# Hybrid decoder layer on one core: four z tiles of the first branch move between the memory's key products, and the token combinations and the first pair's weights are made beside them

## The chip, the cores and the metric

The kernel runs on one core of a Trainium2 chip. The metric is the device time of one execution in microseconds; of several runs the median counts. The core has an engine for matrix products (PE, with its weight loads as PEld), a vector engine (DVE), a scalar engine (ACT), a general engine (POOL), and SP, which here issues all DMA transfers, in order.

## The reference, cut to what matters

The layer normalises 1024 tokens of width 1024 to `h` and multiplies `h` by one wide matrix `w_in`. Its columns feed three branches: a gated delta rule over chunks (8 heads), a causal attention with two maps per head (8 heads), and an attention into a fixed memory of 256 rows (4 heads). The parts that the change touches:

```python
(gdn_qkv, gdn_a, gdn_b, gdn_z, dq, dk, dv, dz, mq, mz, gate_logits) = [h @ w_in[:, lo:hi] for lo, hi in bounds]
...
oa = gated_delta_rule_chunked(qa, ka, va, g, beta)
oa = rms_norm(oa, gdn_norm_w) * jax.nn.silu(gdn_z.reshape(b, s, GDN_HEADS, GDN_DV))
...
m = rms_norm(mem, mem_norm_w)
mk, mv = jnp.split(m @ w_mem_kv, 2, axis=-1)
```

After the branches, gates merge them, an output product and a last normalisation follow, and `x` is added.

## The kernel before, in words

All products are made in float32 precision out of halves: every operand is split into a rounded part (hi) and the rest (lo), and each product is three passes: hi by hi, hi by lo, lo by hi.

**Weights.** `wsplit` (L159) takes a raw tile of 128x512 (tag `wr`, three buffers), lets SP load it (L163, 256 KB), casts it on ACT (L165, tag `wh`, two buffers) and subtracts on DVE (L167, tag `wl`, two buffers). Every weight outside the paired products goes through these buffers, one after the other: this text calls the three of `wr` the ring.

**Stage 1, up to L709.** The delta rule. Inside `with gx:` two pools, `yp` and `gp`, hold its tiles. `gemm` (L207) makes a tile of 128 columns by 1024 tokens in 48 matmuls out of two raw tiles. Beside the gemms run Python generators: `spawn` adds one, `tick` advances each by a step, and `count` ticks after every six matmuls. `scan` (L632) is the recurrence, three steps per chunk, eight chunks, two heads at a time; after it POOL normalises (L689, L690) and `channels` (L244) transposes the result to a tile `os[n]`. `zmul(n)` (L263) makes z tile n with a gemm, takes silu on ACT (L267), multiplies `os[n]` by it (L270) and stores it. Tiles 0 to 5 stand here, with their silu in a `yt` tile of pool `yp`; then `flush` ends all generators, and `gx` closes.

**Stage 2, L711 to L1024.** A new pool `xp` takes the place of the closed ones: its tiles exist only when those of `yp` and `gp` are given up. `mem_norm` (L735) loads the memory, normalises and transposes it into hi and lo tiles. Beside it `zmul(6)` and `zmul(7)` run. `combine_tokens` (L802) makes, in four rounds, the sums and differences of token blocks that Strassen's scheme needs (L808 to L817) and splits them (L732, L733), in tiles of tags `hi`, `lo`, `o` and `q`; the tiles `os[n]` are of tag `q` too, eight buffers. Then come 8 key tiles (`mem_keys`, L767: two raw tiles each, 12 matmuls of 256 columns per raw tile), whose results are stored (L1016), and `mem_values` (L778) for f = 0 and f = 1: 8 raw tiles each, 6 matmuls of 512 columns per raw tile, and the results are split from PSUM and stored by eight DMAs after each f (L1023).

**Stage 3, from L1028.** `strassen` (L876) makes the rest of the wide product in pairs of column tiles, seven products per pair instead of eight. `Pair.load` (L834) loads raw weights, `Pair.upper` (L841) makes a weight sum on DVE (L850, in a tile of the ring) and casts it (L852), `Pair.lower` (L854) subtracts (L856), `Pair.multiply` (L858) does the matmuls. Before its loop it loads the first pair and makes three uppers and two lowers: products 1, 5 and 6. The sum for product 6 uses that for 5, and the sum for product 3, made in the loop, reads that for 6. Attention runs as a generator beside it. PSUM accumulators of stage 2 are given up and new banks opened (L1291) before the pairs.

**What sets the order.** The order of the text is a priority. Each engine's queue is put in order when the kernel is built: of what is ready by the builder's own clock, the instruction first in the text goes first, and one further down goes where the others are not ready or their buffers not free. On the chip each queue then runs strictly in that order.

Of the kernel before, what the change touches and what calls it, by code (L numbers as in the profile page):

```python
# [19 lines left out]
KT = D // P  # L20
NT = S // P
H = 8
# [7 lines left out]
C_Z = 3088  # L30
# [20 lines left out]
def hybrid_layer_kernel(  # L51
# [124 lines left out]
    def spawn(gen):  # L176
        threads.append(gen)
# [85 lines left out]
    def zmul(n, zcol, tile_):  # L263

        pz = gemm(w_in, zcol + n * P, hh, hl)
        sz = tile_()
        A.activation(sz, pz, AF.Silu)  # L267
        until(lambda: n in os)
        o = os.pop(n)
        V.tensor_tensor(o, o, sz, op=ALU.mult)  # L270
        nc.sync.dma_start(oscr[0][n], o)


    with gx:
# [428 lines left out]
        for step, h in ((key, 0), (key, 1), (key, 2), (key, 3), (qry, 0), (val, 0), (qry, 1), (val, 1),  # L703
                        (val, 2), (key, 4), (val, 3), (key, 5), (qry, 2), (key, 6), (qry, 3), (key, 7),
                        (val, 4), (val, 5), (qry, 4), (qry, 5), (val, 6), (val, 7), (qry, 6), (qry, 7)):
            step(h)
        for n in range(6):
            zmul(n, C_Z, yt)
        flush()  # L709

# [24 lines left out]
    def mem_norm():  # L735

        mts = []
        for t in range(2):
            mt = rtile((P, D))
            nc.sync.dma_start(mt, mem[t * P:(t + 1) * P, :])  # L740
            mts.append(mt)
        for _ in range(2):
            mh.append(xtile((P, 4, MEM), F32R))
            ml.append(xtile((P, 4, MEM), F32R))
        sq = rtile()
        for mt in mts:
            ss = small([P, 1], "ss", 4)
            A.activation(sq, mt, AF.Square, accum_out=ss)
            rs = small([P, 1], "rs", 4)
            rpow(rs, ss, 1.0 / D, EPS, mhalf)  # L750
            V.tensor_scalar(mt, mt, rs, None, op0=MUL)
            yield
        for k2 in range(4):
            pt = sd()
            for kk in range(2):
                for t in range(2):
                    T.transpose(pt[:, 2 * kk + t], mts[t][:, (2 * k2 + kk) * P:(2 * k2 + kk + 1) * P], ident)
            for kk in range(2):
                k = 2 * k2 + kk
                src = pt[:, 2 * kk:2 * kk + 2].rearrange("p a b -> p (a b)")  # L760
                A.activation(mh[k // 4][:, k % 4], src, AF.Copy, scale=memw[:, k:k + 1])
                V.scalar_tensor_tensor(ml[k // 4][:, k % 4], src, memw[:, k:k + 1],
                                       mh[k // 4][:, k % 4].bitcast(F32), op0=MUL, op1=SUB)
            yield
        ready.add("mem")

    def mem_keys(n, mk):  # L767
        pm = acc()
        for j in range(2):
            hi, lo = wsplit(wcols(w_kv, j, n * P))  # L770
            for kk in range(4):
                T.matmul(pm[:, :MEM], lhsT=hi[:, kk], rhs=mh[j][:, kk], start=(j + kk == 0), stop=False)
                T.matmul(pm[:, :MEM], lhsT=hi[:, kk], rhs=ml[j][:, kk], start=False, stop=False)
                T.matmul(pm[:, :MEM], lhsT=lo[:, kk], rhs=mh[j][:, kk], start=False, stop=(j == 1 and kk == 3))
                count(2)
        split(mk[0][:, n % 4], mk[1][:, n % 4], pm[:, :MEM])
# [25 lines left out]
    def combine_tokens():  # L802

        for j in range(4):
            (b1, (u0, u1)), (b2h, b2l) = lower[j], upper[j]
            b11, b12, b21, b22 = (hit((P, 512), F32) for _ in range(4))
            f32 = lambda t: t.bitcast(F32)
            V.tensor_tensor(b11, f32(b1[:, 0]), f32(b1[:, 1]), op=ADD)  # L808
            V.tensor_tensor(b12, f32(u0[:, :]), f32(u1[:, :]), op=ADD)
            for b, sl in ((b21, slice(0, 512)), (b22, slice(512, 1024))):  # L810
                V.tensor_tensor(b, f32(b2h[:, sl]), f32(b2l[:, sl]), op=ADD)
            yield
            t2 = lot((P, 512), F32)
            V.tensor_tensor(b11, b12, b11, op=SUB)
            V.tensor_tensor(t2, b22, b11, op=SUB)
            V.tensor_tensor(b12, b22, b12, op=SUB)
            V.tensor_tensor(b21, b21, t2, op=SUB)  # L817
            yield
            for p, src, new in ((5, b11, ot), (6, t2, ot), (7, b12, qt), (4, b21, qt)):
                t = new((P, 2, 512), F32R)  # L820
                split(t[:, 0], t[:, 1], src)
                comb[p].append((t[:, 0], t[:, 1]))
                yield

    ORDER = (1, 5, 6, 2, 7, 3, 4)

# [47 lines left out]
                self.put(i, f, ps, self.kept.get(add))  # L874

    def strassen(pairs):  # L876
        seq = [(q, p) for q in pairs for p in ORDER]

        def upper(n):
            if n < len(seq):  # L880
                seq[n][0].upper(seq[n][1])

        def lower(n):
            if n < len(seq):
                seq[n][0].lower(seq[n][1])

        pairs[0].load(True)
        pairs[0].load(False)
        upper(0)
        lower(0)  # L890
        upper(1)
        lower(1)
        upper(2)
        for n, (q, p) in enumerate(seq):
            if p in (1, 6) and n + 7 < len(seq):
                seq[n + 7][0].load(p == 1)
            lower(n + 2)
            upper(n + 3)
            q.multiply(p)
# [78 lines left out]
    def key_query(h):  # L978
        return Pair((C_DK + h * P, C_DQ + h * P),
                    gathered(lambda i, f, t: spawn((queries_apart if i else keys_apart)(h, f, t))))  # L980

    def values_pair(h):
        def done(i, f, t):
            nc.sync.dma_start(vd[h + i][:, half[f]], t)
            mark("v", h + i)
        return Pair((C_DV + h * P, C_DV + (h + 1) * P), gathered(done))
# [11 lines left out]
    def silu_z(bi, col, n):  # L998
        return Pair((col + n * P, col + (n + 1) * P), through(True, szd[bi][n:n + 2], ("sz", bi, n // 2)))

    def gates(bi, n):
        c = C_G + bi * D + n * P
        return Pair((c, c + P), through(False, gts[bi][n:n + 2], ("gate", bi, n // 2)))

    spawn(mem_norm())
    zmul(6, C_Z, xtile)
    zmul(7, C_Z, xtile)
    until(lambda: "mem" in ready)
    spawn(combine_tokens())
    for n in range(2):  # L1010
        mk = [xtile((P, 4, MEM), F32R) for _ in range(2)]
        for i in range(4):
            mem_keys(4 * n + i, mk)
        for h in range(2):
            for u in range(2):
                nc.sync.dma_start(mkd[2 * n + h][:, :, u], mk[u][:, 2 * h:2 * h + 2].bitcast(F32))  # L1016
    mv = [[xtile((P, D), F32R) for _ in range(2)] for _ in range(2)]
    for f in range(2):
        mem_values(f, mv)
        for h in range(2 * f, 2 * f + 2):  # L1020
            for t in range(2):
                for u in range(2):
                    nc.sync.dma_start(mvd[h][:, t, u], mv[t][u][:, h * MEM:(h + 1) * MEM].bitcast(F32))  # L1023
# [253 lines left out]
        ready.add("attention")  # L1277
        yield from make0

    pairs = []  # L1280
    for h in range(H):
        pairs.append(key_query(h))
        pairs.append(silu_z(1, C_DZ, h - 1) if h % 2 else values_pair(h))
    for h in range(4):
        pairs.append(mem_query(h))
        pairs.append(silu_z(2, C_MZ, 2 * h))
    pairs += [gates(b, n) for b in range(3) for n in range(0, KT, 2)]

    spawn(attention())
    pace[0] = 2  # L1290
    new_banks()  # L1291
    strassen(pairs)
    new_banks()
    ready.add("pairs")
    pace[0] = 6
# [68 lines left out]
    pw = xtile()  # L1364
    nc.sync.dma_start(pw, post_w.to_broadcast([P, D]))

    def products(po, t, ks, f):
        ts_ = slice(t * P, (t + 1) * P)
        for k in ks:
            for lt, rt in ((yh, wh), (yh, wl), (yl, wh)):  # L1370
                T.matmul(po[f], lhsT=lt[k][:, ts_], rhs=rt[k][f],  # L1371
                         start=(k == 0 and lt is yh and rt is wh), stop=(k == 7 and lt is yl))
# [4 lines left out]
    pos = {t: columns() for t in range(2)}  # L1377
    for t in range(2):
        for f in range(2):
            products(pos[t], t, range(4), f)  # L1380
    for t in range(NT):

        ts_ = slice(t * P, (t + 1) * P)
        po = pos[t] if t < 2 else columns()
        xr, res = xtile(), xtile()
        nc.sync.dma_start(xr, x[ts_, :])
        ss = small([P, 2], "oss", 4)
        for f, sl in enumerate(half):
            products(po, t, range(4 if t < 2 else 0, KT), f)
            A.activation(res[:, sl], po[f], AF.Square, scale=1.0 / 32, accum_out=ss[:, f:f + 1])  # L1390
        rs = small([P, 1], "rs", 4)
        V.tensor_scalar(rs, ss[:, 0:1], ss[:, 1:2], EPS, op0=ADD, op1=ADD)
        G.tensor_tensor(rs, rs, mhalf[:, 0:1], op=ALU.pow)
        for f, sl in enumerate(half):
            V.scalar_tensor_tensor(res[:, sl], po[f], rs, pw[:, sl], op0=MUL, op1=MUL)
            (V if f else G).tensor_tensor(res[:, sl], res[:, sl], xr[:, sl], op=ADD)
            nc.sync.dma_start(out[ts_, sl], res[:, sl])
# [24 lines left out]
```

## Time and profile before

| what | value |
|---|---|
| median of 3 runs | 1966.76 us (1961.39 to 1967.66) |
| the profiled execution's own time | 1959.28 us |
| its span, first to last instruction | 1957.3 us |
| PE busy | 1889.6 us of the span |
| mean granted clock of TensorE | 0.993 of full |

The profile is of one execution, which took 1959.28 us, 0.4% under the median; 2.0 us of it lie outside the span. All times of the trace below count from the span's start. The stages touched lie between 505 and 627 us.

### The profile page before, as it was taken

The page shows a single profiled execution, that of the slowest core. Times are in us where ns is not written, and L with a number is a line of the kernel's source. Part 1 is how long each engine was busy: PE and PEld are TensorE (multiplying, and loading weights), DVE is VectorE, ACT ScalarE, POOL GpSimd, SP SyncE. Part 2 cuts the span into 40 slices and gives each one's busy share as a digit, 9 for nine tenths or more (in the row PEclk, how much of TensorE's full clock was granted, in tenths as well). Part 3 has the DMA queues.
Part 4 walks back from the last instruction along what each step waited for, and adds up shares of the span by engine and source line. Part 5 has one row for each costly group of instructions (what it writes and reads, how often), then busy time and mean ns, then how long its engine had stood idle before and what let it go on. Part 6 is the DMA issues. An engine that isn't in the chain of part 4 may idle for free.

```text
span 1957.3 us, 28521 instructions
## 1 busy us (share of the span) xinstructions
PE 1889.6 (97%) x10231; PEld 1561.1 (80%) x10231; DVE 1261.3 (64%) x2578; ACT 931.1 (48%) x2057; POOL 140.5 (7%) x115
## 2 busy tenths in 40 slices
PE   7999999999988999999999999999999999999998
PEld 5778888788875787878887878888878777888886
DVE  6787678754395687878877777766666653434532
ACT  5544554554363565656655555655444551212211
POOL 1230131302101000000000000000000000000011
PEclk9999999999999999999999999999999999999999
DMA  4323131321264646555555354443476477665522
GB/s 126 95 85 101 43 91 52 102 64 55 83 197 143 200 150 205 153 180 158 183 157 172 113 158 162 143 151 108 162 235 201 146 240 254 202 206 165 159 86 86
DMA packets 292609, 282.44 MB, mean 144 GB/s; under 512 B 40066, under 2 KB 224756, under 8 KB 292468
## 3 DMA queue, kind: packets, MB, share of 16 engines
q1 hardware_dynamic: 292468, 280.63, 45.9%
q8 instruction: 80, 1.31, 0.3%
q14 instruction: 61, 0.50, 0.1%
HBM read 189.27 MB, written 91.29 MB: 143 GB/s over the span
## 4 chain that ended last, share of the span: by engine, by line
PE 77%; DVE 8%; DMA 5%; issue 5%; ACT 3%; POOL 2%; SPq 1%; DVEq 0%; POOLq 0%; ACTq 0%
PE bank L866 30%; PE acc L217 9%; PE acc L222 9%; PE acc L218 9%; PE sd L1154 3%; PE sd L1108 2%; PE sd L1109 2%; PE sd L1142 2%; PE sd L1213 1%; DMA x<-mqd 1%; PE sd L1371 1%; DMA wr<-in_w_mem_kv_dram 1%; PE sd L472 1%; DVE u L973 1%; DVE wl L167 1%
## 5 line engine op out<-in xcount | busy, mean ns | idle before, releaser
L866 PE MATMUL bank<-h,hi 128*128 128x512 f32 x864 | 284.9, 402 | 2.8 <-DVE x L733 2.8
L217 PE MATMUL acc<-h,wh 128*128 128x512 f32 x548 | 225.2, 412 | 4.4 <-DVE y L435 3.0
L165 ACT CAST wh<-wr 128x512 fp32r<-128x512 f32 x144 | 89.3, 620 | 285.2 <-PE acc L218 247.0
L218 PE MATMUL acc<-h,wh 128*128 128x512 f32 x548 | 215.6, 394 | 0.0
L866 PE MATMUL bank<-o,hi 128*128 128x512 f32 x576 | 190.7, 404 | 1.6 <-ACT u L871 1.5
L866 PE MATMUL bank<-q,hi 128*128 128x512 f32 x576 | 189.9, 403 | 2.3 <-DVE u L921 2.2
L866 PEld LDWEIGHTS bank<-h,hi 128*128 128x128 f32 x864 | 160.6, 189 | 35.9 <-issue 3.2
L222 PE MATMUL acc<-h,wl 128*128 128x512 f32 x548 | 181.8, 394 | 0.6 <-DVE wl L167 0.6
L866 PE MATMUL bank<-h,lo 128*128 128x512 f32 x432 | 173.5, 402 | 0.0
L167 DVE TENSOR_TENSOR wl<-wr,wh 128x512 fp32r<-128x512 f32 x144 | 103.7, 722 | 105.7 <-ACT wh L165 99.7
L852 ACT CAST hi<-wr 128x512 fp32r<-128x512 f32 x144 | 89.3, 620 | 125.5 <-PE bank L866 124.6
L856 DVE TENSOR_TENSOR lo<-wr,hi 128x512 fp32r<-128x512 f32 x144 | 99.8, 693 | 56.5 <-PE bank L866 48.6
L866 PEld LDWEIGHTS bank<-q,hi 128*128 128x128 f32 x576 | 107.0, 189 | 25.2 <-DVE u L921 2.6
L866 PEld LDWEIGHTS bank<-o,hi 128*128 128x128 f32 x576 | 107.4, 190 | 24.0 <-ACT u L871 2.4
L217 PEld LDWEIGHTS acc<-h,wh 128*128 128x128 f32 x548 | 103.4, 189 | 23.2 <-issue 4.4
L222 PEld LDWEIGHTS acc<-h,wl 128*128 128x128 f32 x548 | 102.7, 188 | 22.7 <-DVE wl L167 1.3
L218 PEld LDWEIGHTS acc<-h,wh 128*128 128x128 f32 x548 | 103.6, 189 | 16.9 <-DVE h L733 0.3
L866 PE MATMUL bank<-o,lo 128*128 128x512 f32 x288 | 116.4, 404 | 0.0
L866 PE MATMUL bank<-q,lo 128*128 128x512 f32 x288 | 115.7, 402 | 0.0
L1124 ACT ACTIVATE x<-x,ng 128x256 f32<-128x256 f32 (+7 forms) x128 | 98.7, 774 | 31.8 <-DVE ng L1120 31.4
L852 ACT CAST hi<-raw 128x512 fp32r<-128x512 f32 x108 | 67.0, 620 | 75.0 <-PE bank L866 72.6
L866 PEld LDWEIGHTS bank<-h,lo 128*128 128x128 f32 x432 | 81.7, 189 | 16.3
(361 smaller groups left out, 4048.4 us busy)
## 6 DMA issues: line engine op xcount, KB each, us to landing
raw<-in_w_in_dram SPq DMA_DIRECT2D x144, 256.0 KB, 3.6
wr<-in_w_in_dram SPq DMA_DIRECT2D x64, 256.0 KB, 2.9
qd<-u SPq DMA_DIRECT2D x64, 256.0 KB, 3.1
wl<-qd SPq DMA_DIRECT2D x64, 256.0 KB, 3.7
gts<-u SPq DMA_DIRECT2D x48, 256.0 KB, 3.3
u<-oscr SPq DMA_DIRECT2D x48, 256.0 KB, 4.7
raw<-gts SPq DMA_DIRECT2D x24, 512.0 KB, 4.4
o<-gscr SPq DMA_DIRECT2D x16, 512.0 KB, 4.4
```

The costliest lines, as they stand in the source:

```text
L165: A.copy(hi, raw)
L167: V.tensor_tensor(lo, raw, hi.bitcast(F32), op=ALU.subtract)
L217: T.matmul(ps[:, sl], lhsT=hi[:, kk], rhs=hh(k, f), start=(k == 0), stop=False)
L218: T.matmul(ps[:, sl], lhsT=hi[:, kk], rhs=hl(k, f), start=False, stop=False)
L222: T.matmul(ps[:, sl], lhsT=lo[:, kk], rhs=hh(k, f), start=False, stop=(k == 7))
L852: A.copy(self.hi[p], self.src[p])
L856: V.tensor_tensor(self.lo[p], self.src[p], self.hi[p].bitcast(F32), op=SUB)
L866: T.matmul(ps, lhsT=t[l][:, kk], rhs=comb[p][kk][r], start=(first and kk + n == 0), stop=(kk == 3 and n == 2), skip_group_check=True)
L1108: T.matmul(ps[m], lhsT=q4[:, m], rhs=ks[m][:, u:e], start=True, stop=False)
L1109: T.matmul(ps[m], lhsT=q4[:, 2 + m], rhs=ks[m][:, u:e], start=False, stop=True)
L1124: A.activation(s[i][m][:, :w], s[i][m][:, :w], AF.Exp, bias=ng[:, m:m + 1], scale=scl, accum_out=l)
L1154: T.matmul(po[:, 0], lhsT=pT[:, c], rhs=vt[:, c], start=(c == 0), stop=(c == i))
```

## The change

The z tiles 4 and 5 leave stage 1: they come after `gx` has closed, beside `mem_norm` and the token combinations, with their silu in an `xp` tile. Tile 6 comes after the second of the eight key tiles, tile 7 after the sixth. `combine_tokens` starts with `mem_norm`, but its round j waits until no more than 6 - 2j tiles `os[n]` are left, since it needs their buffers. `strassen` becomes a generator that stops once after its preparation, and is called up to there between the value products of f = 0 and f = 1; the list of pairs moves up for that. The products' own count is the same. A helper `products` near the end is renamed `out_products`.

```diff
@@ stage 1
-        for n in range(6):
+        for n in range(4):
             zmul(n, C_Z, yt)
         flush()
@@ combine_tokens
         for j in range(4):
+            while len(os) > 6 - 2 * j:
+                yield
...
                 comb[p].append((t[:, 0], t[:, 1]))
                 yield
+        ready.add("tokens")
@@ strassen
         upper(1)
         lower(1)
         upper(2)
+        yield
         for n, (q, p) in enumerate(seq):
@@ stage 2
     spawn(mem_norm())
-    zmul(6, C_Z, xtile)
-    zmul(7, C_Z, xtile)
+    spawn(combine_tokens())
+    zmul(4, C_Z, xtile)
+    zmul(5, C_Z, xtile)
     until(lambda: "mem" in ready)
-    spawn(combine_tokens())
     for n in range(2):
         mk = [xtile((P, 4, MEM), F32R) for _ in range(2)]
         for i in range(4):
             mem_keys(4 * n + i, mk)
+            if i == 1:
+                zmul(6 + n, C_Z, xtile)
...
     for f in range(2):
+        if f:
+            until(lambda: "tokens" in ready)
+            products = strassen(pairs)
+            next(products)
         mem_values(f, mv)
@@ stage 3
     spawn(attention())
     pace[0] = 2
     new_banks()
-    strassen(pairs)
+    for _ in products:
+        pass
     new_banks()
```

## Rows read from the trace of the kernel before

**Rows 1.** The page's part 1: busy time, share of the span, instructions.
```profile
PE 1889.6 (97%) x10231; PEld 1561.1 (80%) x10231; DVE 1261.3 (64%) x2578; ACT 931.1 (48%) x2057; POOL 140.5 (7%) x115
```

**Rows 2.** Stretches, 504.7 to 626.6 us: length, then each engine's busy time, clock.
```profile
core 0: us, PE busy (x) PEld busy (x) DVE busy (x) ACT busy (x) POOL busy (x), PEclk, DMA share, GB/s
...
504.70:533.40 28.70, 28.70 (x153) 24.23 (x152) 8.42 (x19) 10.26 (x26) 7.50 (x4) 1.00 0.24 74
533.40:558.00 24.60, 23.56 (x111) 19.15 (x110) 23.10 (x40) 13.92 (x26) 1.87 (x2) 1.00 0.63 193
558.00:586.20 28.20, 24.13 (x184) 22.10 (x182) 26.46 (x46) 15.91 (x31) 0.00 (x0) 1.00 0.67 205
586.20:601.60 15.40, 13.87 (x58) 9.92 (x59) 9.75 (x16) 6.73 (x12) 0.00 (x0) 1.00 0.59 173
601.60:619.90 18.30, 13.12 (x49) 8.40 (x48) 12.03 (x20) 8.43 (x15) 6.40 (x4) 1.00 0.56 178
619.90:626.60 6.70, 3.91 (x9) 3.15 (x10) 1.98 (x3) 1.16 (x2) 0.00 (x0) 0.50 0.46 159
```

**Rows 3.** PE's waits, 533.4 to 623 us: total, times, longest.
```profile
PE acc L785 <- ACT wh L165: 4.6, 4, 2.3
PE bank L866 <- DVE x L733: 2.8, 1, 2.8
PE acc L786 <- DVE nlam L1038: 2.1, 1, 2.1
```

**Rows 4.** Timeline of DVE, chunks of the scan: start, length, line, operation, tiles, count.
```profile
492.31 0.35 DVE L651 SCALAR_TENSOR_TENSOR v<-sd,negeG,v 128x128 f32<-128x128 f32 x1 [2.11 <-PE sd L648]
...
498.91 0.35 DVE L651 SCALAR_TENSOR_TENSOR v<-sd,negeG,v 128x128 f32<-128x128 f32 x1 [1.98 <-PE sd L648]
```

**Rows 5.** Timeline of POOL after the last scan.
```profile
517.04 1.64 POOL L689 TENSOR_TENSOR sso<-sso,mhalf 128x8 f32<-128x8 f32 x1 [45.05 <-DVE sso L688]
...
522.80 1.90 POOL L690 TENSOR_TENSOR v<-v,sso 128x1024 f32<-128x1024 f32 x1
```

**Rows 6.** Timeline of DVE, from z tile 5 to the normalised memory.
```profile
534.30 1.23 DVE L270 TENSOR_TENSOR q<-q,y 128x1024 f32<-128x1024 f32 x1 [0.23 <-ACT y L267]
...
535.63 0.69 DVE L808 TENSOR_TENSOR hi<-h 128x512 f32<-128x512 f32 x1
...
552.19 0.48 DVE L762 SCALAR_TENSOR_TENSOR x<-sd,cols,x 128x256 fp32r<-128x256 f32 x1
```

**Rows 7.** Timeline of PE: two products of a key tile, two of a value tile.
```profile
558.00 0.28 PE L772 MATMUL acc<-x,wh 128*128 128x256 f32 x1
558.12 0.28 PE L773 MATMUL acc<-x,wh 128*128 128x256 f32 x1
...
591.26 0.39 PE L785 MATMUL acc<-wh,x 128*128 128x512 f32 x1
591.49 0.40 PE L786 MATMUL acc<-wl,x 128*128 128x512 f32 x1
```

**Rows 8.** Chain of waits, one turn of the ring: start, length, what.
```profile
590.20 3.98 DMA wr<-in_w_mem_kv_dram
594.28 0.63 ACT wh L165
594.93 0.70 DVE wl L167
595.65 3.22 DMA wr<-in_w_mem_kv_dram
```

**Rows 9.** Timeline of SP's queue, 594 to 612 us.
```profile
595.65 6.06 SPq L163 DMA_DIRECT2D wr<-in_w_mem_kv_dram  x5
...
602.46 3.87 SPq L1023 DMA_DIRECT2D mvd<-x  x8
606.37 1.42 SPq L163 DMA_DIRECT2D wr<-in_w_mem_kv_dram  x3
```

**Rows 10.** Timeline of DVE in the value products of f = 1.
```profile
613.99 1.52 DVE L856 TENSOR_TENSOR lo<-wr,hi 128x512 fp32r<-128x512 f32 x1
```

More of the change, by code (lines that the diff above doesn't have):

```diff
@@ L1003, in gates @@
         return Pair((c, c + P), through(False, gts[bi][n:n + 2], ("gate", bi, n // 2)))
+    pairs = []
+    for h in range(H):
+        pairs.append(key_query(h))
+        pairs.append(silu_z(1, C_DZ, h - 1) if h % 2 else values_pair(h))
+    for h in range(4):
+        pairs.append(mem_query(h))
+        pairs.append(silu_z(2, C_MZ, 2 * h))
+    pairs += [gates(b, n) for b in range(3) for n in range(0, KT, 2)]
     spawn(mem_norm())
-    zmul(6, C_Z, xtile)
-    zmul(7, C_Z, xtile)
+    spawn(combine_tokens())
+    zmul(4, C_Z, xtile)
+    zmul(5, C_Z, xtile)
     until(lambda: "mem" in ready)
-    spawn(combine_tokens())
     for n in range(2):
@@ L1278, in attention @@
         yield from make0
[L1280 to L1287, printed above, removed]
     spawn(attention())
@@ L1365, in hybrid_layer_kernel, with out_products @@
     nc.sync.dma_start(pw, post_w.to_broadcast([P, D]))
-    def products(po, t, ks, f):
+    def out_products(po, t, ks, f):
         ts_ = slice(t * P, (t + 1) * P)
@@ L1379, in hybrid_layer_kernel @@
         for f in range(2):
-            products(pos[t], t, range(4), f)
+            out_products(pos[t], t, range(4), f)
     for t in range(NT):
@@ L1388, in hybrid_layer_kernel @@
         for f, sl in enumerate(half):
-            products(po, t, range(4 if t < 2 else 0, KT), f)
+            out_products(po, t, range(4 if t < 2 else 0, KT), f)
             A.activation(res[:, sl], po[f], AF.Square, scale=1.0 / 32, accum_out=ss[:, f:f + 1])
```

## The prediction

> **What bounds the kernel now.** I read the busy shares first: PE is busy 97% of the span [rows 1], so the change can only win PE's idle time, or time at the half clock. Then I cut the span into stretches around the edited lines [rows 2]. The reader is to see that PE is full from 504.7 to 533.4 (z tiles 4 and 5 beside the end of the last scan), idle 1.0 us in the next 24.6 (z tiles 6 and 7, the memory's normalisation), and then idle 4.1, 1.5 and 5.2 us in the key products, in the value products of f = 0 and in those of f = 1. In the last stretch TensorE's granted clock is 0.50, its 1.2 GHz level, right after such gaps. DVE is nearly full from 533.4 to 586.2. The waits say what PE lacks: the cast of the next weight tile, a lo part behind other DVE work, and, at the change to the pairs, the splitting of the last value tile [rows 3].
>
> Two pitches turn this into losses. A key product follows the last by 0.12 us, a value product by 0.23 [rows 7]; so the 12 products of a raw key tile take 1.44 us and the 6 of a raw value tile 1.40. From 558.0 to 601.6 there are 16 raw key tiles and 8 raw value tiles: 23.0 + 11.2 = 34.2 us of work in 43.6, a loss of 9.4. From 601.6 to 619.9 there are 8 more: 11.2 in 18.3, a loss of 7.1.
>
> One turn of the ring is a load of about 3.4 us (3.98 in the row; the chain's next is 3.2), an issue of 0.33, a cast of 0.63 and a subtraction of 0.70 [rows 8], some 5.05. With three raw tiles that is 1.68 us per tile, already more than PE's 1.4; the measured pitch is 43.6 / 24 = 1.82.
>
> **The change, part by part.** No product is added or removed.
>
> A. Tiles 4 and 5 leave stage 1. The work of 504.7 to 533.4 stays on PE: tile 4's products are free to fill the gaps of the last scan, since only their silu needs the new pool. What moves is the pool's gate. Now it opens when tile 5's product with `os` ends at 535.5, and DVE's first token sum starts 0.1 us later [rows 6]. Then it opens after the last scan: POOL needs 7.66 us from its first power to its last product [rows 5], and the transposes that read the result about 1 us. The scan's two last chunks run at 6.6 us each [rows 4], of which 18 z products at 0.23 are 4.1. Bounds for the tail: as now (POOL starts at 517.0), or 5.4 us earlier if the chunks shrink to their own chain of some 3.9 us (an estimate: six hops, PE and DVE in turn, of two instructions of about 0.3 us each); I take the middle, 514.3, because fillers still stand between the steps. So the gate opens at 523.0 (520.3 to 525.7), 12.5 us earlier than now. But the memory's tiles take 17.1 us from the gate, 535.5 to 552.7 [rows 6], and nothing but tiles 4 and 5 covers them: PE's work up to the end of the first key tile is 533.4 + 1.3 (transposes) + 2.9 = 537.6, and that tile cannot end before 523.0 + 17.1 + 0.4 = 540.5. A new wait of 2.9 us, less the 1.0 that goes: **+1.9 us** (-0.8 to +4.6). Queued behind it on PE are the key products, and nothing else is ready, since tile 6's weights come behind theirs in the ring.
>
> B. Tiles 6 and 7 between the keys. A z tile's two raw tiles keep PE 24 x 0.23 = 5.5 us each, so behind it the ring stands full: one tile split and three raw, four in stock. The runs without z are 4, 8 and 12 tiles long (keys 0-1; 2-5; 6-7 and f = 0); beyond the stock lie 0 + 4 + 8 = 12 tiles, each losing 1.82 - 1.42 = 0.40: a loss of 4.8 against 9.4, **-4.6 us**. Bounds: by the ring's own turn alone (1.68) the loss is 3.1, a gain of 6.3; with a stock of two, 18 tiles lose 7.2, a gain of 2.2. The token sums (32 sums and 16 splits in four rounds) lie beside it: two rounds under tiles 4 and 5, where DVE is busy 8.4 of 28.7 us [rows 2], the third by tile 6, the fourth beside keys 6 and 7. I cost them at nothing; without that cover they would come back as late lo parts. The Trainium skill, page "Perfetto Trace Analysis", section "Optimization Strategy", says that stages with different most-contended engines may gain by being interleaved; taken alone it would give all 9.4 us back and a sum of -3.9. The ring's turn speaks against that beyond the stock.
>
> C. The first pair's preparation, moved in front of f = 1. Its two sums use the ring, and the sum for product 6 is kept until the sum for product 3 is made, inside the pair loop and behind all of f = 1 in the ring. So f = 1 has two raw tiles. Now five loads go out from 595.65 to 601.7, four of them for f = 1, before eight stores hold SP from 602.46 to 606.3 [rows 9]. Then the two slots that come free first go to the sums, and the loads start at about 599.2 and 600.4: the first product is at 603.6 (2.0 late), the next two loads wait for the stores until 606.4 (PE idle 4.0 to 610.4), and after that each pair of tiles needs a turn of 4.7 us: pairs start at 615.1 and 619.8, the end is at 622.6 instead of 619.9, **+2.7 us**. In it the wait of 2.1 us [rows 3], for a lo part behind the pair's own lo part [rows 10], is gone. Bounds: the loads of f = 1 take their slots first and that wait goes with some of the others, -3.2; or every tile costs half a turn, 8 x 2.5 + 3.9 = 23.9, +5.6. What DVE did at 611 to 619 is not missed later: the wait for the banks (2.8) [rows 3] stays, as the last value tile is split as before.
>
> D. Clock. The half clock after 619.9 costs (626.6 - 619.9 - 2.8) / 2 = 2.0 us [rows 2, 3] and stays. New gaps, in A and C, can bring another such stretch; 6.7 us at half clock cost at most 3.3. I take **+0.9**, 0 to 3.3.
>
> Sum: 1.9 - 4.6 + 2.7 + 0.9 = +0.9 us. On the profiled execution, 1959.3 becomes 1960.2; that execution is 7.5 us under the median, and the median's 1966.8 becomes **1967.7**. 0.3% is 5.9 us, about what a measurement of this kernel can tell from no change.
>
> **Rivals.**
>
> 1. *The interleaving works in full.* The ring is full whenever PE needs it, the memory is ready in time, and f = 1 keeps its loads: -0.8 - 6.3 - 3.2 = -10.3, 1956.5. For it: DVE is full exactly where PE waits now [rows 2], and half of DVE's load moves away. Against: the ring's turn and the slots of C. It is what the Trainium skill's rule on interleaving, named in B, would promise.
>
> 2. *The ring with one tile held becomes the bound of f = 1.* Place: the eight loads of f = 1. Price: +5.6 of C's upper end and, as PE idles half the time, a half clock of +3.3; with A and B as taken 1.9 - 4.6 + 5.6 + 3.3 = +6.2, 1973.0. It decides once f = 1 takes more than about 23 us from its first product's due time to its last. For it: the held sum has no other place. Against: if the loads overtake the sums, nothing is held. The Trainium skill, same page and section, says that the same gap repeating can mean that buffers for the next tile are missing. Here the gaps of 2.3 us and less in front of the casts [rows 3] fit that, and the change takes a buffer away.
>
> 3. *It doesn't do what it says.* The queues are put in order by readiness, so tile 6 or 7 may be drawn out from between the keys; then B gives nothing and the sum is +5.5, 1972.3, at the edge of what can be told.
>
> **How the numbers follow.** My forecast's chance is 0.33, rival 1 has 0.31, rival 2 0.28, rival 3 0.08. Rival 1 lies below -5.9 us: faster 0.31. The forecast and rival 3 lie within: same 0.41. Rival 2 is slower: 0.28. All lower bounds together give -10.3, all upper ones 4.6 - 2.2 + 5.6 + 3.3 = +11.3, 1978.1, which hardly come together; I take 1956 to 1976, which holds rival 1 near its edge and rivals 2 and 3 inside. The forecast's own range is 1962 to 1972.
>
> **What would show it.** In the new trace: z products between the second and third and between the sixth and seventh key tile (else rival 3); the first token sum near 523; a wait of about 3 us on PE before the first key product (A); keys and f = 0 with under 5 us of idle time (B); two loads instead of four before SP's eight stores, and f = 1 over 20 us long (C). If f = 1 is under 16 us, or no key waits for the memory, the sum is wrong on the slow side. A stretch at 0.50 before the pairs would price D.

## The result and the profile after

The changed kernel takes **1980.55 us** (median of 6 runs, 1977.73 to 1982.09); the kernel before, beside it on the same chip, 1962.59 (6 runs, 1959.15 to 1967.66). The ratio is 1.0086, 95% interval 1.0069 to 1.0104: slower by some 17 us (the medians lie 18.0 apart). The prediction was 1967.7 with a range up to 1976, and "same" as its likeliest case. It was wrong.

The profiled execution took 1980.78 us, its span is 1977.9, 20.6 more than before. The page's part 1 answers to [rows 1]: the count of products is the same, and PE is busy 10 us longer at a lower mean granted clock, 0.986 instead of 0.993.

```profile
PE 1900.0 (96%) x10231; PEld 1567.8 (79%) x10231; DVE 1261.5 (64%) x2578; ACT 931.8 (47%) x2057; POOL 140.4 (7%) x115
```

First find a common point. The silu of z tile 3 is the last thing that both kernels make the same way. Its row in the timeline of ACT, of the kernel before and then of the changed one:

```profile
505.00 1.03 ACT L267 ACTIVATE y<-acc 128x1024 f32<-128x1024 f32 x1
```
```profile
508.29 1.03 ACT L267 ACTIVATE y<-acc 128x1024 f32<-128x1024 f32 x1
```

So 3.3 us of the 20.6 arose in code that is the same in both. The first product of a pair starts at 622.69 before and at 643.20 after. This "edited stretch", from that silu to that product, took 117.7 us and takes 134.9: **+17.2 us**, about the whole loss of the medians. From there to the end the two need 1334.6 and 1334.7.

The stretches of the changed kernel, answering to [rows 2] (same columns: length, busy time by engine, clock, DMA):

```profile
508.30:521.30 13.00, 10.54 (x64) 8.44 (x62) 5.88 (x15) 4.55 (x17) 3.60 (x3) 1.00 0.23 80
521.30:527.70 6.40, 4.80 (x19) 4.08 (x20) 0.00 (x0) 2.07 (x3) 3.42 (x2) 0.50 0.01 4
527.70:541.90 14.20, 13.38 (x64) 10.36 (x63) 13.00 (x25) 9.60 (x20) 1.87 (x2) 0.99 0.51 153
541.90:550.20 8.30, 0.50 (x2) 0.30 (x2) 8.30 (x15) 2.78 (x5) 0.00 (x0) 0.70 0.36 119
550.20:557.30 7.10, 7.09 (x20) 5.64 (x21) 7.07 (x12) 2.04 (x4) 0.00 (x0) 0.63 0.25 74
557.30:603.90 46.60, 45.51 (x288) 40.88 (x286) 27.28 (x44) 19.92 (x36) 0.00 (x0) 1.00 0.56 168
603.90:617.80 13.90, 12.59 (x50) 8.46 (x48) 8.33 (x13) 6.88 (x12) 0.00 (x0) 1.00 0.55 172
617.80:640.20 22.40, 16.68 (x48) 10.84 (x48) 10.08 (x17) 7.39 (x12) 6.71 (x4) 0.85 0.53 159
```

and PE's waits from 508 to 645 us, answering to [rows 3] (the pairs' L866 is L869 now, and of the lines named below L1023 is L1043; L808 to L817 are L810 to L819):

```profile
PE acc L222 <- DVE wl L167: 7.8, 1, 7.8
PE acc L785 <- ACT wh L165: 4.3, 4, 1.6
PE sd L250 <- POOL v L690: 4.1, 2, 2.5
PE bank L869 <- DVE x L733: 3.0, 1, 3.0
```

Three things are new. **At 541.9** PE does 0.50 us of work in 8.3, while DVE is busy for all 8.3: one wait of 7.8 us for a rest part. **From 518.8** PE waits twice for POOL, 2.5 and 1.6 us, and from 521.3 it stands at its 1.2 GHz level, 0.50, for 6.4 us. **From 617.8** f = 1 takes 22.4 us instead of 18.3. One thing is better: from 557.3 to 617.8 PE hardly idles. Those 60.5 us hold z tiles 6 and 7 too, 96 products at 0.23 us or 22.1; the rest is 38.4 us where before it was 43.6.

Why PE waits at 541.9 stands in DVE's queue. ACT cast the second raw tile of z tile 5 at 535.15 (first row, timeline of ACT), so its rest part could be made from 535.8. The other rows are DVE's timeline:

```profile
535.15 0.61 ACT L165 CAST wh<-wr 128x512 fp32r<-128x512 f32 x1
```
```profile
527.76 0.69 DVE L810 TENSOR_TENSOR hi<-h 128x512 f32<-128x512 f32 x1 [8.47 <-PE sd L250]
...
537.05 0.69 DVE L733 TENSOR_TENSOR q<-hi,q 128x512 fp32r<-128x512 f32 x1
537.65 0.69 DVE L810 TENSOR_TENSOR hi<-h 128x512 f32<-128x512 f32 x1
...
548.26 1.29 DVE L733 TENSOR_TENSOR q<-hi,q 128x512 fp32r<-128x512 f32 x2
549.47 1.29 DVE L167 TENSOR_TENSOR wl<-wr,wh 128x512 fp32r<-128x512 f32 x2
```

The rest part (L167) runs at 549.47, 13.7 us after it could, behind two rounds of token sums (L810 to L819) and their splits (L733). Nobody needs the sums before f = 1 is prepared; z5's remaining products, and behind them all of PE's queue, need L167. DVE had stood idle for 8.47 us until 527.76, waiting for the gate: the sums can't use the time before it.

### The profile page after: what moved, and what is told of

It reads as the page before. It is cut to its first block, busy times and chain, and to the rows that moved or that the text cites. A ratio compares the mean times of both kernels' runs of the same rounds, so it can differ in the third digit from the quotient of the medians.

```text
span 1977.9 us, 28520 instructions
## 1 busy us (share of the span) xinstructions
PE 1900.0 (96%) x10231; PEld 1567.8 (79%) x10231; DVE 1261.5 (64%) x2578; ACT 931.8 (47%) x2057; POOL 140.4 (7%) x115
## 4 chain that ended last, share of the span: by engine, by line
PE 76%; DVE 9%; DMA 5%; issue 4%; ACT 2%; POOL 2%; SPq 1%; DVEq 0%; POOLq 0%; ACTq 0%
PE bank L869 30%; PE acc L222 9%; PE acc L217 9%; PE acc L218 9%; PE sd L1174 3%; PE sd L1128 2%; PE sd L1129 2%; PE sd L1162 1%; DMA x<-mqd 1%; PE sd L1233 1%; PE sd L1383 1%; DMA wr<-in_w_mem_kv_dram 1%; PE sd L472 1%; DMA u<-szd 1%; DVE u L978 1%
## 5 line engine op out<-in xcount | busy, mean ns | idle before, releaser
L869 PE MATMUL bank<-h,hi 128*128 128x512 f32 x864 | 285.1, 403 | 3.0 <-DVE x L733 3.0
L869 PE MATMUL bank<-o,hi 128*128 128x512 f32 x576 | 190.2, 403 | 1.9 <-ACT u L874 1.9
L869 PE MATMUL bank<-q,hi 128*128 128x512 f32 x576 | 189.7, 403 | 2.0 <-DVE u L926 1.8
L869 PEld LDWEIGHTS bank<-h,hi 128*128 128x128 f32 x864 | 160.6, 189 | 36.0 <-issue 3.4
L167 DVE TENSOR_TENSOR wl<-wr,wh 128x512 fp32r<-128x512 f32 x144 | 104.3, 726 | 112.6 <-ACT wh L165 106.7
L869 PE MATMUL bank<-h,lo 128*128 128x512 f32 x432 | 173.6, 402 | 0.0
L869 PEld LDWEIGHTS bank<-q,hi 128*128 128x128 f32 x576 | 107.0, 189 | 24.7 <-DVE u L926 2.3
L869 PEld LDWEIGHTS bank<-o,hi 128*128 128x128 f32 x576 | 107.2, 190 | 24.1 <-ACT u L874 2.8
L869 PE MATMUL bank<-o,lo 128*128 128x512 f32 x288 | 116.0, 403 | 0.0
L869 PE MATMUL bank<-q,lo 128*128 128x512 f32 x288 | 115.9, 402 | 0.0
L869 PEld LDWEIGHTS bank<-h,lo 128*128 128x128 f32 x432 | 81.8, 189 | 16.1
```

What stands on the lines that cost most here:

```text
L167: V.tensor_tensor(lo, raw, hi.bitcast(F32), op=ALU.subtract)
L869: T.matmul(ps, lhsT=t[l][:, kk], rhs=comb[p][kk][r], start=(first and kk + n == 0), stop=(kk == 3 and n == 2), skip_group_check=True)
```

## The experiments

All ratios are to the kernel of before, run beside each on the same chip. "Stretch" is the edited stretch of the one profiled execution, 117.7 us before; a difference of a us or two between two of them says little by itself. Here z4 is z tile 4, and so on. Line numbers are those of the changed kernel. e3, e4, e6 and e12 are called the kernel of before, and have its order but for what is named; of the changed text they keep the generator, the place of the list of pairs and the condition on the rounds.

| run | what differs | ratio (95%) | stretch, us |
|---|---|---|---|
| the change | | 1.0086 (1.0069 to 1.0104) | 134.9 |
| e1 | change, sums later | 1.0035 (1.0017 to 1.0054) | 126.3 |
| e2 | change, preparation later | 1.0078 (1.0056 to 1.0100) | 130.3 |
| e5 | change, z4 and z5 back | 1.0101 (1.0080 to 1.0123) | 137.1 |
| e6 | before, z6 and z7 between keys | 1.0075 (1.0054 to 1.0095) | 130.1 |
| e7 | e1 and e2 together | 1.0016 (1.0002 to 1.0030) | 120.6 |
| e3 | before, preparation early | 1.0024 (1.0013 to 1.0036) | 123.2 |
| e4 | before, sums early | 1.0044 (1.0029 to 1.0059) | 131.1 |
| e9 | e7, z4 back | 1.0027 (1.0010 to 1.0044) | 122.3 |
| e12 | e3, the first pair's sums in a tile of their own | 0.9994 (0.9981 to 1.0007) | 117.6 |
| e10 | before, sums behind the keys | 1.0002 (0.9990 to 1.0015) | 117.6 |
| e11 | e7, sums behind the keys | 1.0018 (1.0003 to 1.0033) | 121.7 |
| e8 | change, sums on POOL | 1.0156 (1.0132 to 1.0179) | 150.1 |
| e13 | e7, scan's tail shorter | 1.0007 (0.9990 to 1.0024) | 118.4 |
| e14 | before, scan's tail shorter | 1.0000 (0.9985 to 1.0016) | 119.1 |
| e15 | change with three mends | 0.9988 (0.9974 to 1.0002) | 116.7 |

**e1: the sums behind the z tiles in the text.**

```diff
-    spawn(combine_tokens())
     zmul(4, C_Z, xtile)
     zmul(5, C_Z, xtile)
     until(lambda: "mem" in ready)
+    spawn(combine_tokens())
```

> The changed kernel (1980.6 us), with the token sums started again only when the memory is ready, as before the change; z4 and z5 stay behind the scan's tail, z6 and z7 between the keys, the pair preparation early. Theory 'cover' (the sums stand in VectorE's queue ahead of the rest parts of z5's weights, which costs the wait of 7.8 us and about 2.6 us at half clock): the wait on the rest part falls under 2 us and the time falls by 8 to 10 us, to about 1971-1973. Rival 'place' (what costs is that only four z tiles stand ahead of POOL's last transposes and of the gate, whatever VectorE does): within 2 us of the changed kernel, 1979-1982. Rival 'ring' (the loss sits in the held raw tile of the last value products): no change, 1980-1981.

Measured 1.0035, 0.51% or 10 us under the change; no wait for L167 stands in front of z5's products any more. The first round of sums still starts right at the gate (524.16), where nothing else is ready. But the timeline of DVE shows the rest part of z5's second raw tile at 530.97, ahead of what is left of that round, and the next rest part ahead of the second round:

```profile
530.97 0.68 DVE L167 TENSOR_TENSOR wl<-wr,wh 128x512 fp32r<-128x512 f32 x1
...
539.60 0.68 DVE L167 TENSOR_TENSOR wl<-wr,wh 128x512 fp32r<-128x512 f32 x1
540.20 0.69 DVE L810 TENSOR_TENSOR hi<-h 128x512 f32<-128x512 f32 x1
```

All sums are still made. So it is the sums' priority, not their amount.

**e4: the same from the other side.** In the kernel of before, the sums alone go ahead of z6 and z7:

```diff
     spawn(mem_norm())
+    spawn(combine_tokens())
     zmul(6, C_Z, xtile)
     zmul(7, C_Z, xtile)
     until(lambda: "mem" in ready)
-    spawn(combine_tokens())
```

> The kernel of before with one part alone: the token sums stand ahead of z6 and z7 in the text, so they have priority over the rest parts of z6's and z7's weights; z4 and z5 in the first stage, no z between the keys. Theory 'cover' (priority over rest parts on VectorE is what costs, wherever z tiles stand beside the sums): PE waits some 5 to 8 us for a rest part of z6 or z7 and follows with half clock: ratio 1.003 to 1.005. Rival 'only with the z tiles of the change' (before, the sums run in the same place without harm, as the memory tiles hold them back): ratio 0.999 to 1.001. Rival 'gain' (the sums are done before the keys need VectorE, and the keys get faster): ratio 0.997 to 0.999.

Measured 1.0044, as "cover" said, and PE's waits show the same line, now for a raw tile of z6:

```profile
PE acc L222 <- DVE wl L167: 7.3, 1, 7.3
```

**e8: the sums' 32 additions on POOL** (`G.tensor_tensor` for `V.tensor_tensor` in L810 to L819).

> The changed kernel with the additions and subtractions of the token combinations (eight 512-column instructions per round, 32 in all) on POOL instead of VectorE; their splits stay on VectorE. Place and priority in the text are as in the changed kernel (1980.6, ratio 1.0086). Theory 'cover' (VectorE's time ahead of z5's rest part is what costs): two rounds of some 4.9 us less on VectorE ahead of that rest part, so the wait of 7.8 us falls to 0 to 4 us, ratio 1.003 to 1.006. Rival 'place' (it is the sums' tiles or their order, not VectorE's time): 1.008 or more. Rival 'POOL is slow' (its additions take several times VectorE's 0.69 us, and the sums are late for the preparation that waits for them): above 1.009, with the wait moved to the call between f = 0 and f = 1.

The wait for z5's rest part is gone, which "cover" allowed for, but the time is 1.0156, in the range of "POOL is slow". The place is not the one that this rival named: the new wait comes ahead of the keys and not at the call between f = 0 and f = 1. Groups of POOL, then one wait each of DVE and of PE, in the edited stretch ("issue" stands where the profile shows nothing that PE waited for):

```profile
L813 POOL TENSOR_TENSOR hi<-h,h 128x512 f32<-128x512 f32 x8 | 11.0, 1376 | 7.1 <-DVE q L733 5.0 <-DVE rp L155 1.5 <-ACT o L732 0.7
```
```profile
DVE raw L751 <- POOL rs L156: 7.1, 2, 5.4
```
```profile
PE sd L757 <- issue: 10.3, 1, 10.3
```

An addition takes POOL 1.38 us (up to 1.73 on other lines) where DVE needs 0.69, and the memory's normalisation, which takes one small power on POOL per tile (L156), now queues behind them. The powers come so late that the memory's transposes (L757), which read what DVE makes with them (L751), start 37.5 us after z3's silu instead of 26.6. The Trainium skill, page "GPSIMD Engine Reference", section "Elementwise — side-by-side cycle accounting", gives an addition of 2048 columns as 1.96 times slower there than on VectorE; the rows here, at 512 columns, give 2.0 to 2.5. The run moved the mistake to another queue.

**e3, e2 and e12: the early preparation.** e3 is the kernel of before with `products = strassen(pairs); next(products)` called ahead of f = 1; e2 is the change without that.

> The kernel of before with one part alone: the first pair's preparation is called between the value products of f = 0 and f = 1. Theory 'ring' as in my step C: the held sum leaves two raw tiles, f = 1 takes 21 to 22.5 us instead of 18.3: 2.7 to 4 us more, ratio 1.0014 to 1.002. Rival 'moved, not saved': ratio 0.9995 to 1.0005. Rival 'the sums must be done first' (the call waits for all token sums, which in this order are late): VectorE's queue delays the value weights, ratio above 1.003.

> The changed kernel (1980.6 us) without the early preparation of the first pair: its loads and first weights come after the value products, as before the change. Theory 'cover' and theory 'ring' agree that the last value products go back from 22.4 to about 18.3 us; 'cover' puts 4 us of the loss there, so about 1976.5 (-4). 'Ring' puts most of the loss there, so 1968 or less. Rival 'moved, not saved' (the preparation costs its time wherever it stands, and only shifts it from the value products to the wait before the first pair): within 1.5 us of the changed kernel.

e3 measures 1.0024, 4.7 us: the loss that "ring" forecast, a little above its 1.002, which lies inside the interval. e2's ratio, 0.08% under the change, is inside the intervals and tells nothing alone; its stretch is 4.6 us shorter than the change's. What the cost is, e12 tells: e3, with the sums for products 5 and 6 of the first pair outside the ring.

```diff
-                self.src[p] = wp.tile([P, 4, P], F32, name=nm("wr"), tag="wr", bufs=3)
+                if p in (5, 6) and self is pairs[0]:
+                    self.own = getattr(self, "own", None) or xtile((P, 2, 4, P))
+                    self.src[p] = self.own[:, p - 5]
+                else:
+                    self.src[p] = wp.tile([P, 4, P], F32, name=nm("wr"), tag="wr", bufs=3)
```

> The kernel of before with the early preparation alone, as in the run with that part alone (ratio 1.0024, f = 1 21.7 us instead of 18.2), but the first pair's sums for products 5 and 6 lie in a tile of their own instead of two tiles of the ring. Theory 'ring' (the tile held for product 3 and the slots that the sums take are the loss): f = 1 back to 18.3 us or less, ratio 0.9995 to 1.0005. Rival 'queues' (the preparation's four loads on SP, casts on ACT and subtractions on VectorE stand ahead of the value weights): f = 1 stays at 21 us or more, ratio 1.0018 or more. Half and half: 1.001.

Measured 0.9994, no loss: "ring". The stretch of f = 1, in e3 and then in e12, from the end of f = 0 (e3's 21.7 in the expectation counts from its own first product):

```profile
606.00:629.30 23.30, 15.97 (x48) 10.35 (x48) 9.57 (x17) 7.29 (x12) 6.56 (x4) 0.85 0.49 153
```
```profile
604.90:622.40 17.50, 14.73 (x49) 9.56 (x47) 12.66 (x21) 8.35 (x14) 5.81 (x4) 0.90 0.60 187
```

and SP's queue, in the changed kernel (the answer to [rows 9]) and in e12:

```profile
606.82 10.43 SPq L163 DMA_DIRECT2D wr<-in_w_mem_kv_dram  x6
618.44 3.76 SPq L1043 DMA_DIRECT2D mvd<-x  x8
622.25 0.94 SPq L163 DMA_DIRECT2D wr<-in_w_mem_kv_dram  x2
...
626.71 7.53 SPq L163 DMA_DIRECT2D wr<-in_w_mem_kv_dram  x4
```
```profile
593.35 11.76 SPq L163 DMA_DIRECT2D wr<-in_w_mem_kv_dram  x8
605.71 4.36 SPq L1045 DMA_DIRECT2D mvd<-x  x8
610.11 1.61 SPq L163 DMA_DIRECT2D wr<-in_w_mem_kv_dram  x3
...
614.83 0.33 SPq L163 DMA_DIRECT2D wr<-in_w_mem_kv_dram  x1
```

Behind the eight stores (`mvd`) the change has six of the eight loads of f = 1 still to make, e12 four. In e12 TensorE's granted clock is 0.90 in f = 1, and the stretch is still no longer than the 18.3 us of before.

**e5 and e6: what the z tiles cover.** e5 is the change with z4 and z5 in stage 1 again; e6 is the kernel of before with `zmul(6)` and `zmul(7)` moved between the keys and nothing else.

> The changed kernel (1980.6 us) with z4 and z5 made again in the first stage, ahead of POOL's last transposes; token sums still start with the memory's normalisation, z6 and z7 stay between the keys, the pair preparation stays early. Theory 'cover': no z weights are split while the first sums run, so the 7.8 us wait cannot come, and the 4.1 us of waits of the transposes on POOL with some 2 us at half clock go too; but nothing stands beside the memory's normalisation, whose chain (15 to 17 us from the gate) then shows partly as a wait of TensorE, some 8 to 12 us: about 1972-1976. Rival 'place' (the order of z4 and z5 is the whole loss): 1963 or below. Rival 'sums anywhere' (VectorE's queue of sums delays whatever key weights come next just as it delayed z5's): 1980 or above.

> The kernel of before with one part of the change alone: z6 and z7 go between the keys, everything else (z4 and z5 in the first stage, token sums after the memory is ready, pair preparation after the value products) as before. Nothing then covers the memory's normalisation, which the two z tiles covered before. Theory 'cover' (interleaving gains 5 us in the keys, the uncovered memory chain costs more): two z tiles of 11 us fall away ahead of the keys, the chain of 15 to 17 us is bare but for the transposes: 5 gained, 2 to 8 lost against the kernel of before (1962.6): 1960-1967. Rival 'interleaving is all': 1957-1958. Rival 'the z tiles only change places' (keys as slow with z between as without): 1968-1975.

Both missed what "cover" said: at the 1962.6 us that the expectations start from, 1.0101 is 1982 us instead of 1972 to 1976, and 1.0075 is 1977 instead of at most 1967, above every rival. The place of the loss is the one that "cover" named; the times that it gave are too low. With no z tile beside the memory's normalisation PE waits in front of the memory's transposes, and the clock goes down; e5's time is that of the rival "sums anywhere", but its longest wait is this one too (10.7), not one for a rest part. PE's longest wait in e6, then two of its stretches:

```profile
PE sd L757 <- ACT raw L748: 10.7, 1, 10.7
```
```profile
534.20:556.00 21.80, 9.74 (x44) 8.05 (x42) 14.72 (x26) 8.61 (x16) 1.89 (x2) 0.73 0.39 120
555.00:562.00 7.00, 6.71 (x33) 6.18 (x33) 5.42 (x11) 3.54 (x8) 0.00 (x0) 0.56 0.65 161
```

So two z tiles are worth more beside the normalisation than between the keys (e6), and moving z4 and z5 there was not the mistake: without them the change is no faster (e5; the intervals of the two overlap).

**e7, e9, e11: what is left when both are undone.** e7 takes e1's and e2's edits together; e9 moves z4 back as well; e11 is e7 with `spawn(combine_tokens())` behind the key loop.

> The changed kernel with two parts undone together: the token sums after the memory is ready, and the first pair's preparation after the value products. What stays of the change: z4 and z5 behind the scan's tail, z6 and z7 between the keys. Theory 'cover' (three separate costs that add: sums in VectorE's queue 10 us, held raw tile 1.6 to 4, POOL wait and half clock about 7 against a gain of 5 in the keys): the late sums were worth 0.51% and the late preparation 0.08%, so 0.15 to 0.3% above before, some 3 to 6 us. Rival 'one cost' (both parts take the same idle time away, so undoing both is worth no more than undoing the sums): 0.35% above, as the late sums alone. Rival 'place is free' (the z tiles' new places gain their 5 us in full): 0.2 to 0.3% below before.

> As the kernel with late sums and late preparation, and z4 too goes back into the first stage; what stays is z5 beside the memory's normalisation and z6 and z7 between the keys. Theory 'cover': z4 ahead of POOL's last transposes takes the wait on POOL (4.9 us) and its half clock (about 2) away; z5 alone, 11 us, covers less of the memory's chain of 15 us, so a bare wait of 3 to 5 us with some half clock comes in its place: within 0.2% of the kernel with both late, that is ratio 1.000 to 1.003. Rival 'only POOL's wait costs': 0.996 to 0.998, faster than before. Rival 'the memory's chain decides' (its cover is z4 and z5 both): 1.005 or more, towards the bare chain that the kernel with z4 and z5 both back showed (1.0075).

> The kernel with late sums and late preparation (ratio 1.0016: z4 and z5 behind the scan's tail, z6 and z7 between the keys), with the token sums still later, behind the keys in the text. Theory 'cover': a little better than with the sums right behind the memory, as the keys' rest parts (0.7 us of waits) come first: 1.0005 to 1.0015; POOL's wait of 4.9 us and its half clock stay. Rival 'too late': above 1.0025. Rival 'the keys gain their full 9 us': 0.998.

e7 measures 1.0016, so the parts add up: the sums alone cost 0.44% (e4), the preparation alone 0.24% (e3), the z tiles' places 0.16% (e7), together 0.84% against the change's 0.86%. Each has an interval of 0.1 to 0.15% either way, so the sum is no closer than that. e9 (1.0027) and e11 (1.0018) lie within e7's interval: neither z4's place nor still later sums are shown to mend what is left. e9's time is in the range of "cover", but not by its mechanism: PE still waits 3.8 us for POOL, and no wait of 3 to 5 us for the memory comes in its place.

**e10: the sums still later, in the kernel of before.**

> The kernel of before with one part moved the other way: the token sums stand behind the eight key tiles in the text, so every rest part of a key weight has priority over them. Theory 'cover' (priority of the sums over rest parts on VectorE costs wherever both are due): the keys' waits for rest parts (1.2 us) and some of the waits for casts (1.4) go, the sums fill VectorE's gaps and run on into the value products: ratio 0.9985 to 0.9995. Rival 'the sums come too late' (they reach into the last value products and hold the first pair up): ratio above 1.001. Rival 'VectorE has no part in the keys of before' (the ring's turn alone bounds them): 0.9997 to 1.0005.

Measured 1.0002: no change, the third case of the expectation. There the sums' place behind the memory's tiles already costs nothing.

**e13, e14, e15: the scan's tail, and all mends together.** In e7 the transposes of the last two heads still wait 4.9 us for POOL. e13 gives their last product to DVE, which is idle there; e14 does that to the kernel of before.

```diff
-                G.tensor_tensor(vs[h], vs[h], bc(sso[h], P), op=ALU.mult)
+                (V if h >= 6 else G).tensor_tensor(vs[h], vs[h], bc(sso[h], P), op=ALU.mult)
```

> The kernel with late sums and late preparation (ratio 1.0016), with the last two heads' normalising product moved from POOL (1.9 us each, behind 1.64 us each for the power) to VectorE, which stands idle there. Theory 'tail' (the transposes that wait for POOL are the rest of the loss): the last product ends some 2.7 us earlier, PE's wait falls from 4.9 to 2 us or less and the half clock after it shrinks or goes: ratio 0.9985 to 1.0005. Rival 'memory chain' (the gate opens earlier but the memory's chain or the ring then takes the time): 1.001 to 1.002, as without it. Rival 'VectorE is late for z' : above 1.002.

> Control: the kernel of before with the same two products on VectorE. Before, z4 and z5 lie beside POOL's tail and PE does not wait for it: all theories expect no change, ratio 0.9993 to 1.0007. Should it be faster by more than 0.1%, then what the run beside it gains is no mend of the change.

The stretch up to the gate, in e7 and in e13; z3's silu is later in e13, so the first begins 10.3 us after it and the second 7.4:

```profile
521.30:530.40 9.10, 4.24 (x21) 3.54 (x20) 0.69 (x1) 2.06 (x3) 6.04 (x4) 0.79 0.10 29
```
```profile
521.30:531.10 9.80, 6.89 (x41) 5.43 (x40) 3.60 (x7) 3.23 (x10) 3.66 (x2) 1.00 0.10 28
```

and PE's waits there, in e7 and in e13:

```profile
PE sd L250 <- POOL v L690: 4.9, 2, 2.4
```
```profile
PE sd L250 <- DVE sso L688: 1.6, 1, 1.6
PE sd L250 <- DVE v L690: 1.3, 1, 1.3
```

e13 measures 1.0007 and e14 1.0000. The waits fall to 2.9 us, not quite to the 2 that "tail" forecast, the gate opens 2.2 us earlier after z3's silu, and the half clock there is gone. But 1.0007 lies between "tail" (at most 1.0005) and "memory chain" (at least 1.001), and the 0.09% between e7 and e13 is less than their intervals: the trace shows the mechanism, and the times don't prove its size.

e15 is the change itself with e1's edit, e12's tile and e13's product.

> The change with its three costs mended: token sums behind the memory, the early preparation's two sums in a tile of their own, the last two heads' product on VectorE; z4 and z5 behind the scan, z6 and z7 between the keys, the preparation early. Theory 'three costs' (each was worth what its own run showed, and what is left is the keys' gain of 5 us less what the memory's chain shows): as the short-tail run less 0.03 to 0.06%, ratio 0.998 to 1.000. Rival 'no gain is left': 1.001 or more, so the interleaving would gain nothing even without its side costs.

Measured 0.9988, interval 0.9974 to 1.0002: 0.98% or 19 us better than the change, and with its middle 2 us better than the kernel of before, which the interval doesn't quite secure. So of the 5 us that the interleaving gains at the keys some 2 are left even with all three mends. Its f = 1 runs at the full clock:

```profile
603.60:620.90 17.30, 13.40 (x49) 8.33 (x47) 12.70 (x21) 8.31 (x14) 5.70 (x4) 1.00 0.63 189
```

## Why the prediction was wrong

**The step that failed is in B: "I cost them at nothing; without that cover they would come back as late lo parts."** They came back just so: one wait of 7.8 us, 10 us in all when the sums are taken back (e1), and 8.6 us when they alone are put forward (e4: 0.44% of 1963.75). I had read the cover from a stretch in which DVE is busy 8.4 of 28.7 us [rows 2]. But the sums cannot start before the gate, which lies 19.5 us after z3's silu (527.76 less 508.29). By then PE had 66 products of z4 and z5 left, 15 us, and DVE was busy 21.3 us from there to 550.2, nearly all of it with two rounds of sums and the memory's tiles. And the sums precede z4 and z5 in the text, so the builder put them first. A cost set to nothing also had no upper end: all upper ends together were +11.3, 1978.1, the range was closed at 1976, and the stretch took +17.2.

**A.** POOL's start was as taken: 9.3 us after z3's silu instead of 12.0 [rows 5], 2.7 earlier. That was the middle of two bounds, so that it came out to the tenth is luck. The timeline of POOL:

```profile
517.62 1.64 POOL L689 TENSOR_TENSOR sso<-sso,mhalf 128x8 f32<-128x8 f32 x1 [42.34 <-DVE sso L688]
...
522.90 1.90 POOL L690 TENSOR_TENSOR v<-v,sso 128x1024 f32<-128x1024 f32 x1
```

The gate opened 11.2 us earlier (predicted 12.5), and no key waited for the memory: its tiles took 15.2 us from the gate instead of 17.1, and they were whole at 543.0, inside the wait for the rest part. The prediction's sign for that case, "the sum is wrong on the slow side", did not hold, as other terms outweighed it. What I left out is PE's own queue at that place: the transposes wait twice for POOL, 4.1 us, with z4's products behind them, and then 4.80 us of PE's work at the half clock, worth 2.4. This second omission comes to 6.5 us where the whole of A was put at +1.9.

**B, the interleaving.** Right: z products stand between the second and third and between the sixth and seventh key, and keys and f = 0 take 38.4 instead of 43.6 us, 5.2 less where I said 4.6. Rival 3, that the change doesn't do what it says, falls. So does rival 1. The Trainium skill's rule on interleaving (page "Perfetto Trace Analysis", section "Optimization Strategy") holds in sign for the stretch that is interleaved: 5.2 us of the 9.4 came back. It says nothing of what the moved work had covered elsewhere (e6) or what is put first in a shared queue (e1, e4).

**C.** Right in mechanism, too small: +2.7 predicted, +4.1 in the trace (22.4 against 18.3), +4.7 in the kernel's time alone (e3). Two loads instead of four go out before the stores, and e12 shows that the ring's tiles are all of it. This is rival 2's place and sign; the change is a little short of the 23 us from which it was to decide, e3 with 23.3 a little above. PE's idle time in f = 1 only rose from 5.2 to 5.7 us: most of the +4.1 is busy time at the half clock. But the casts that these products need wait for their loads again and again (timeline of ACT in the changed kernel; before, the one such wait in f = 1 is 3.9):

```profile
625.34 0.62 ACT L165 CAST wh<-wr 128x512 fp32r<-128x512 f32 x1 [4.51 <-DMA wr<-in_w_mem_kv_dram]
...
629.69 0.62 ACT L165 CAST wh<-wr 128x512 fp32r<-128x512 f32 x1 [2.77 <-DMA wr<-in_w_mem_kv_dram]
...
635.22 0.62 ACT L165 CAST wh<-wr 128x512 fp32r<-128x512 f32 x1 [2.87 <-DMA wr<-in_w_mem_kv_dram]
```

So the slow products fill time that the loads would largely have left idle; how much the clock adds of its own no run separates. The Trainium skill, page "Perfetto Trace Analysis", section "Optimization Strategy", says that the same gap repeating can mean that buffers for the next tile are missing. These rows and e12, where f = 1 is back at 17.5 us, agree.

**D.** +0.9 was too little, and so was its upper end of 3.3. Besides the 2.4 us at the gate, the 5.3 us from 550.2 ran at 0.51, behind the wait of 7.8, and two pieces of f = 1 at 0.54 and 0.51, each behind a wait for a load:

```profile
550.20:555.50 5.30, 5.29 (x13) 4.17 (x14) 5.27 (x9) 1.59 (x3) 0.00 (x0) 0.51 0.34 99
555.50:557.30 1.80, 1.80 (x9) 1.47 (x8) 1.80 (x4) 0.45 (x2) 0.00 (x0) 1.00 0.00 0
620.00:623.50 3.50, 3.44 (x9) 2.66 (x9) 1.30 (x3) 0.62 (x1) 0.00 (x0) 0.54 0.82 256
627.00:630.50 3.50, 3.50 (x10) 2.71 (x10) 0.64 (x1) 0.79 (x2) 0.00 (x0) 0.51 0.50 150
```

Half of PE's busy time in such a piece is what the level costs its products: 2.6 us after the long wait, 3.5 in f = 1, where it is part of C's 4.1 and not to be added. The account of the stretch, half clock included: the gate 4.1 + 2.4, z5's rest part 7.8 + 2.6, f = 1 4.1, keys and f = 0 -5.2, together +15.8 of the 17.2; the last 1.4 I can't assign.

## What to carry to other kernels

Work that nobody waits for yet must stand behind, not ahead of, work that the bounding engine waits for, when both share an in-order queue; being ready early gives it no right to go first. When work is said to be hidden, look at the time in which it is really allowed to run, which starts at its gate, and give its cost an upper end, here one round's time on that queue. A tile that moves takes its cover along and a buffer that is kept longer is taken from a ring: price both.

## What was not expected of the hardware

Code that is the same in all these kernels took from 504.7 us (e1) to 513.9 (e2, e13) of the span to reach z3's silu, one execution each: half of the effect under study. The granted clock goes with it: cut into pieces of 10 us up to 510, what the clock lacks of full adds up to 3.4 us in e1, 11.9 in e13 and 8.5 in e2, so pieces at the lower level make up most of the 9.2 us, if not all in e2. Why they come in one execution and not in another no run here shows. A common point is needed before one trace is held against another: e13's profiled execution, 1973.38 us, is slower than e7's, 1971.61, though its edited stretch is 2.2 us shorter.
